# Moving the cached-key products inside four turns, and three set-up transfers to GpSimd's queue, in a hybrid decoder step

## The chip, the core and the metric

The kernel runs on one core of a Trainium2 chip, as one program with one launch. The metric is the device time of one execution in microseconds (us); the median of several executions is compared. One more execution is taken by the hardware profiler, and all rows shown here come from it.

## What is computed

The reference is one inference step of a two-layer decoder, for a prompt of 512 tokens and a sample group of 8 sequences with 8 new tokens each. Cut to what matters here:

```python
# layer 0: dilated window attention, three groups (window, dilation) = (128,1), (512,4), (2048,16)
qkv = (h @ w_qkv).reshape(B, T, 3, 3, 8, 64)            # q, k, v of three groups, 8 heads of 64
q = rope(rmsnorm(qkv[:, :, 0], q_gain), pos)
k = rope(rmsnorm(qkv[:, :, 1], k_gain), pos)
# each query sees keys at distances 0, d, 2d, .. window, in the cache and in the new tokens;
# the three groups are merged by their softmax denominators; then @ w_o
x = x + attention
x = x + (silu(h2 @ w_gate) * (h2 @ w_up)) @ w_down
# layer 1: S5 diagonal complex state-space layer, in 64 groups of 16 channels and 64 states
abar = exp(lam * dt); bbar = ((abar - 1) / lam) * bmat
x_t = abar * x_{t-1} + bbar u_t;  y = Re(C x) + D u;  out = gelu(y) @ w_glu, gated
# and a second swiglu; new caches and states are outputs too
```

## The kernel before

All activations are kept transposed (features on the 128 partitions, 576 tokens along the row), in fp32 precision: each fp32 operand is split into a high half (`whi`, rounded, by ScalarE) and a low half (`wlo`, the rest, by VectorE), and each product is three TensorE matmuls. Every weight tile `raw` that SP loads is therefore split by ScalarE and then VectorE before TensorE can use it.

**The QKV stage** (`qkv_phase`, about the first 305 us) runs nine chunks, listed in `CHUNKS` as (part, group) with part 0 = queries, 1 = keys, 2 = values. A chunk is four *turns*, numbered j = 0 to 35; a turn is one weight tile of 256 x 512 against five row banks (four of the prompt, one of the sample), and after each bank comes a *slot*. `begin()` opens a turn: it queues the loads on SP, splits the next weight, runs the work noted for this turn, and returns the split weight. `slot()` runs what was put off by `later(n, fn)`, n slots ahead. All this is written out by hand: VectorE, ScalarE, the SP queue and TensorE's inserted work are kept in program order there. GpSimd's instructions are placed by the planner (the framework's scheduler, which orders the free instructions by a timeline of its own).

After a chunk of queries or keys, the first turn of the next chunk squares its five banks (`square(t)`: a square on ScalarE into `t1`, which has two buffers, then a sum on VectorE into `sh`), one a slot; the second turn takes the root (`rsqrt`) and rotates the banks (`finish`), in the order of `TURNS`; each rotated bank is later transposed on TensorE (`turned`, L655).

Beside this, the sample group's scores against cached keys are made. Groups 0 and 1 go through TensorE (`Score`: transposes L566, `ks` copied by ScalarE, matmuls L578 and L583, then masking `row_out`). Group 2 has one key in sixteen for each query row, so it is done on VectorE: a cache tile `kc` times the query rows `qb` (both 128 x 1024, loaded by SP from the cache and from `qscr`), then a sum over the head dimension into `P2`. There are 32 such pairs, spread over turns by `PAIRS`; each is loaded one turn ahead. When the four pairs of a sequence are done, `Close2` is put off by some slots; it transposes `P2` on TensorE (L416) and masks. Its score accumulator `Sd` has one buffer. The tiles `kc` of all kinds share six buffers (`KST`).

**The first FFN** (`ffn`, about 410 to 880 us) is bound to TensorE. Between its matmul groups a generator `ssm_setup` is advanced (`tick`) that builds the tables of the state-space layer: E (GpSimd multiplies, into `ee`), W (TensorE and ScalarE), T (VectorE) and V (GpSimd, six operations for each of eight f). Each table is written to HBM; `consts(f, q)` loads the four tables of one f back by queue q. The scratch of the f loop (`cb`, `wr`) lies where `ee` was, so it can be written only when E's store is done. Here the planner orders all engines and queues. Beside the tables GpSimd multiplies the gate (`gt`, L1029) and adds the squares of the norm (`ssum`, L194). `pace` mixes copies of old cache rows to the outputs (`o_kv_s`) into the weight loads on SP. SP also carries every load of weights; four `raw` buffers hold them.

Of the kernel before, what the change touches and what calls it, by code (L numbers as in the profile page):

```python
# [8 lines left out]
F32 = mybir.dt.float32  # L9
# [4 lines left out]
OP = mybir.AluOpType  # L14
AX = mybir.AxisListType
# [19 lines left out]
CHUNKS = ((0, 2), (1, 2), (2, 2), (0, 1), (1, 1), (0, 0), (1, 0), (2, 0), (2, 1))  # L35
# [388 lines left out]
def qkv_phase(nc, tc, A, es, L):  # L424
    v, s, g, te = nc.vector, nc.scalar, nc.gpsimd, nc.tensor
# [33 lines left out]
    prods = {}  # L459
    queue, now = [], [0]  # L460

    def later(ahead, fn):
        queue.append((now[0] + ahead, fn))
# [30 lines left out]
    def close(c):  # L494
        if busy[0]:
            later(1, lambda: close(c))
        else:
            c.turn()

    busy = [False]  # L500

    def begin():
        j = turn[0]
        if 4 <= j + 2 < 36:
            part, gi = CHUNKS[(j + 2) // 4]
            raw = L["ring"].tile([128, 2, 512], F32, name="raw", bufs=4)
            kept(nc.sync.dma_start(raw, dram(A["w_qkv"], (j + 2) % 4 * 256 * 4608 + (part * 3 + gi) * 512, [[4608, 128], [128 * 4608, 2], [1, 512]])))
            raws.append(raw)
        for gi in SCORES.get(j, ()):
            b = fill[gi].pop(0)  # L510
            if gi == 1:
                cached.append((gi, b, [cache_tile(nc, A, kst, "kc", gi, b, c0, 2, 0, kept) for c0 in (0, 2)]))
            else:
                t = kst.tile([128, 2, 512], F32, name="kc")
                kept(nc.sync.dma_start(t, dram(A[CACHES[0]], b * WIN[0] * 1024, [[1024, 128], [WIN[0] * 1024, 2], [1, 512]])))
                cached.append((gi, b, [t[:, 0:1]]))
                cached.append((gi, fill[gi].pop(0), [t[:, 1:2]]))
        due = [ready.pop(0) for _ in range(PAIRS.get(j, 0))]
        for _ in range(PAIRS.get(j + 1, 0)):
            b, part = fill[2].pop(0)  # L520
            kc = cache_tile(nc, A, kst, "kc", 2, b, 2 * part, 2, 0, kept)
            qb = kst.tile([128, 2, 512], F32, name="kc")
            kept(nc.sync.dma_start(qb, dram(qscr, (b * 8 + 2 * part) * 512, [[0, 128], [512, 2], [1, 512]])))
            ready.append((b, part, kc, qb))
        if j in notes:
            notes[j]()

        if j < 4:
            split(j)
        if j >= 3:  # L530
            split(j + 1)
        for fn in works.pop(j, ()):
            fn()
        for b, part, kc, qb in due:
            if part == 0:
                prods[b] = dk.tile([128, 4, 4, 8], F32, name="P2")
                g.memset(prods[b], 0.0)
            v.tensor_tensor(kc, kc, qb, OP.mult)
            v.tensor_reduce(prods[b][:, :, 0:2, 2 * part:2 * part + 2].rearrange("p a h c -> p c a h"), kc.rearrange("p c (a h d) -> p c a h d", a=4, h=2),
                            AX.X, OP.add)  # L540
            if part == 3:
                c = Close2(nc, L, v, s, dk, psd, "Sd", prods.pop(b), b)
                later(6 if j > 31 else 10, lambda c=c: close(c))
        return splits.pop(0)

    class Score:
# [532 lines left out]
def ssm_setup(nc, tc, A, L, keep, out):  # L1079
# [26 lines left out]
    with ExitStack() as es:  # L1106
# [169 lines left out]
        with ExitStack() as e2:  # L1276
            wk = e2.enter_context(pool("sse", bufs=1))
            ee = wk.tile([128, 2, 32, 64], F32, name="ee")
            et = [wk.tile([128, 32, 8], F32, name=f"et{i}") for i in range(2)]
            g.tensor_copy(ee[:, :, :, 0], U8[:, :, 0])  # L1280
            for k in range(6):
                n = 2 ** k
                for n0 in range(0, n, 8):
                    w = min(8, n - n0)
                    bc = lambda i: U8[:, i, k][:, :, None].to_broadcast([128, 32, w])
                    cmul(g, ee[:, 0, :, n + n0:n + n0 + w], ee[:, 1, :, n + n0:n + n0 + w], ee[:, 0, :, n0:n0 + w], ee[:, 1, :, n0:n0 + w], bc(0), bc(1), et[0][:, :, :w], et[1][:, :, :w])
                yield
                yield
            yield
            g.tensor_copy(E63, ee[:, :, :, 63])  # L1290
            nc.sync.dma_start(scn["E"].rearrange("f p r q c -> p r f q c"), ee.rearrange("p r (f q) c -> p r f q c", f=8))
            yield
            yield
        with ExitStack() as e2:
# [22 lines left out]
            for f in range(8):  # L1317
                qs = slice(f * 4, f * 4 + 4)
                ps = aux.tile([128, 2, 512], F32, name="aux")
                with tc.issue_after(L["pem"][0].ins):  # L1320
                    for ri in range(2):
                        for q in range(4):
                            te.transpose(ps[:, ri, q * 128:(q + 1) * 128], wr[f][:, ri, q].rearrange("p c s -> p (c s)"), ident)
                wo = wk.tile([128, 2, 4, 128], F32, name="wo")
                s.activation(wo.rearrange("p r q c -> p r (q c)"), ps, AF.Copy)
                nc.sync.dma_start(scn["W"][f], wo)
                yield
                pk = aux.tile([128, 2, 512], F32, name="aux")
                with tc.issue_after(L["pem"][0].ins):
                    for i in range(2):  # L1330
                        for q in range(4):
                            te.matmul(pk[q * 32:q * 32 + 32, 0, :128], cb[i][:, q].rearrange("p a b -> p (a b)"), wr[f][:, i, q].rearrange("p c s -> p (c s)"),
                                      start=i == 0, stop=i == 1, tile_position=(0, q * 32), skip_group_check=True)
                kk = wk.tile([128, 128], F32, name="kk")
                v.tensor_copy(kk, pk[:, 0, :128])
                k7 = kk.rearrange("p (c s) -> p c s", s=8)[:, :, 7]
                v.scalar_tensor_tensor(k7, dmask, dcol[:, f:f + 1], k7, op0=OP.mult, op1=OP.add)
                yield
                with tc.issue_after(L["pem"][0].ins):
                    te.transpose(pk[:, 1, :128], kk, ident)  # L1340
                kt = wk.tile([128, 128], F32, name="kk")
                v.tensor_copy(kt, pk[:, 1, :128])
                st = wk.tile([128, 8, 128], F32, name="st")
                for t in range(8):
                    m = []
                    for p in range(32):
                        c, ss = divmod(p, 8)
                        m.append(c * 8 + (ss + 7 - t if ss <= t else ss))
                    v.stream_shuffle(st[:, t], kt, m)
                if f < 7:  # L1350
                    powers(f + 1)
                yield
                tt = wk.tile([128, 8, 16, 8], F32, name="wo")
                v.tensor_tensor(tt.rearrange("p g c t -> p t (g c)"), st, tmask[:, :, None].to_broadcast([128, 8, 128]), OP.mult)
                nc.sync.dma_start(scn["T"][f], tt.rearrange("p g c t -> p g (c t)"))
                vv = wk.tile([128, 8, 128], F32, name="st").rearrange("p (r q) (c t) -> p r q c t", r=2, c=16)
                vt_ = wk.tile([128, 4, 16, 8], F32, name="vt")
                pw = lambda x: x[:, 1:9, qs].rearrange("p m q -> p q m")[:, :, None, :].to_broadcast(sh)
                cb_ = lambda x: x[:, qs, :, None].to_broadcast(sh)
                p1r, p1i = pw(Ar), pw(Ai)  # L1360
                g.tensor_tensor(vv[:, 0], cb_(Cr), p1r, OP.mult)
                g.tensor_tensor(vt_, cb_(Cn), p1i, OP.mult)
                g.tensor_tensor(vv[:, 0], vv[:, 0], vt_, OP.add)
                g.tensor_tensor(vv[:, 1], cb_(Cn), p1r, OP.mult)
                g.tensor_tensor(vt_, cb_(Cr), p1i, OP.mult)
                g.tensor_tensor(vv[:, 1], vv[:, 1], vt_, OP.subtract)
                for gl in range(2):
                    for ri in range(2):
                        nc.sync.dma_start(scn["V"][f, ri, :, :, gl, :], vv[gl * 64:gl * 64 + 64, ri].rearrange("p q c t -> p q (c t)"))
                yield  # L1370
        consts(0, nc.sync)
        consts(1, nc.sync)
    kp.append(out["es"].enter_context(L["right"]("ssmk1", bufs=2)))
    consts(2, nc.sync)
    consts(3, nc.sync)


def ssm_phase(nc, tc, A, es, L, nin, sp):
# [260 lines left out]
```

## Time and profile before

| | |
|---|---|
| median of 3 runs | 1497.02 us (1496.78 to 1498.91) |
| profiled execution | 1499.43 us, of it 1497.7 us from the first to the last instruction |
| granted TensorE clock | 0.998 |
| busy share | TensorE 98%, VectorE 60%, ScalarE 35%, GpSimd 22% |
| moved by DMA | 322.64 MB, 215 GB/s over the span |
| of it by GpSimd's queue (q0, software) | 3168 packets, 7.48 MB |

How to read the rows: PE is TensorE's matmuls, PEld its weight loads, DVE is VectorE, ACT ScalarE, POOL GpSimd, SP the queue of the sync engine. `out<-in` names the tile written and those read; L12 is line 12 of the kernel; instructions that are kept in order by a wrapper all have line L760. A row of a timeline has the start, the duration, the engine, the line, the operation, the tiles with their shapes, how many, and in brackets the idle time before it with what ended it. A row of the waits has who waited for what, the total in us, the number of waits, the longest. A row of groups has the count, the busy time and the mean in ns, then the idle time before. A row of DMA issues has the size and the median us from issue to landing. A matmul's busy time reaches over the next one's start, as they are pipelined.

### The profile page before, as it was taken

To read this page: it belongs to the slowest core of one execution; us is meant where nothing else is said; L and a number is where in the kernel's file an instruction comes from. 1 tells how busy PE (TensorE), PEld (TensorE's weight loads), DVE (VectorE), ACT (ScalarE), POOL (GpSimd) and SP (SyncE) were. 2 spreads that over 40 slices of the span, in tenths; PEclk is the share of its full clock that TensorE was granted. 3 is DMA by queue.
4 is the path that set the end of the run, shared out by engine and by line. 5 is a ranking of instruction groups with operands and counts; after the bars stand their busy time and mean duration, and the time that the engine had idled before them with its cause. 6 is when DMAs were issued, how large, how long until landed. Compare 5 with 4: busy or idle time off the path is not lost. (4 is left out here: it accounts for less than half of the span.)

```text
span 1497.7 us, 29564 instructions
## 1 busy us (share of the span) xinstructions
PE 1472.2 (98%) x12406; PEld 1384.5 (92%) x12406; DVE 895.8 (60%) x1507; ACT 527.8 (35%) x814; POOL 323.1 (22%) x377
## 2 busy tenths in 40 slices
PE   9999999999999999999999999999999999999998
PEld 7888777777899999999999999899999999999998
DVE  5898988745569545388687768745443323333332
ACT  4534455465552211322223453433432212221222
POOL 2022231320030174134436520201111001100100
PEclk9999999999999999999999999999999999999999
DMA  7566788989875555677867668865555655442212
GB/s 248 209 234 229 237 278 270 365 295 348 247 252 191 204 212 204 245 238 282 288 203 246 221 219 262 232 217 168 186 197 196 223 195 195 137 138 85 83 56 81
DMA packets 191861, 322.64 MB, mean 215 GB/s; under 512 B 40016, under 2 KB 138128, under 8 KB 190320
## 3 DMA queue, kind: packets, MB, share of 16 engines
q1 hardware_dynamic: 183488, 303.24, 60.0%
q10 hardware_dynamic: 5072, 10.04, 2.0%
q0 software_dynamic: 3168, 7.48, 1.5%
q8 instruction: 97, 1.59, 0.4%
q14 instruction: 36, 0.29, 0.1%
HBM read 289.22 MB, written 118.78 MB: 272 GB/s over the span
## 5 line engine op out<-in xcount | busy, mean ns | idle before, releaser
L108 PE MATMUL acc<-xgh,wlo 128*128 128x288 f32 x1760 | 377.9, 296 | 2.2 <-DVE wlo L100 2.2
L108 PE MATMUL acc<-xgh,whi 128*128 128x288 f32 x1760 | 379.1, 297 | 0.1
L108 PE MATMUL acc<-xgl,whi 128*128 128x288 f32 x1760 | 377.7, 296 | 1.0 <-DVE xgl L174 1.0
L100 DVE TENSOR_TENSOR wlo<-raw,whi 128x1024 fp32r<-128x1024 f32 (+1 forms) x166 | 214.9, 1295 | 261.9 <-ACT whi L99 258.4
L99 ACT ACTIVATE whi<-raw 128x1024 fp32r<-128x1024 f32 (+1 forms) x166 | 172.4, 1038 | 476.2 <-PE acc L108 446.0
L108 PEld LDWEIGHTS acc<-xgh,wlo 128*128 128x128 f32 x1760 | 283.2, 188 | 2.7 <-DVE wlo L100 2.5
L108 PEld LDWEIGHTS acc<-xgl,whi 128*128 128x128 f32 x1760 | 283.1, 189 | 1.5 <-DVE xgl L174 1.3
L108 PEld LDWEIGHTS acc<-xgh,whi 128*128 128x128 f32 x1760 | 282.7, 189 | 1.5 <-issue 1.0
L1029 POOL TENSOR_TENSOR gt<-gt,rstd 128x576 f32<-128x576 f32 x44 | 72.9, 1659 | 489.3 <-ACT gt L1028 489.1
L108 PE MATMUL acc<-hh,wlo 128*128 128x288 f32 x704 | 150.8, 295 | 2.1 <-DVE wlo L100 2.1
L108 PE MATMUL acc<-hh,whi 128*128 128x288 f32 x704 | 151.6, 296 | 0.0
L108 PE MATMUL acc<-hl,whi 128*128 128x288 f32 x704 | 150.9, 295 | 0.0
L340 PE MATMUL acc<-whi,xh 128*128 128x512 f32 x288 | 118.8, 414 | 0.5 <-ACT xh L280 0.4
L108 PEld LDWEIGHTS acc<-hh,wlo 128*128 128x128 f32 x704 | 112.9, 188 | 2.3 <-DVE wlo L100 2.3
L108 PEld LDWEIGHTS acc<-hh,whi 128*128 128x128 f32 x704 | 113.0, 188 | 0.6 <-issue 0.6
L108 PEld LDWEIGHTS acc<-hl,whi 128*128 128x128 f32 x704 | 113.1, 188 | 0.0
L340 PE MATMUL acc<-wlo,xh 128*128 128x512 f32 x288 | 112.2, 391 | 0.0
L340 PE MATMUL acc<-whi,xl 128*128 128x512 f32 x288 | 111.5, 393 | 0.0
L1050 DVE TENSOR_TENSOR xT<-acc,xT 128x576 f32<-128x576 f32 x48 | 36.1, 756 | 53.5 <-PE acc L108 53.5
L194 POOL TENSOR_TENSOR ssum<-ssum,sq 128x576 f32<-128x576 f32 x21 | 36.8, 1753 | 136.2 <-ACT sq L193 106.9
L340 PEld LDWEIGHTS acc<-whi,xl 128*128 128x128 f32 x288 | 54.0, 188 | 12.0
L340 PEld LDWEIGHTS acc<-whi,xh 128*128 128x128 f32 x288 | 54.0, 188 | 11.2 <-ACT xh L280 0.9
(395 smaller groups left out, 2008.5 us busy)
## 6 DMA issues: line engine op xcount, KB each, us to landing
o_kv_s<-cache_kv_w SPq DMA_DIRECT2D x64, 1020.0 KB, 6.9
kc<-cache_kv_w SPq DMA_DIRECT2D x100, 512.0 KB, 7.4
raw<-ffn_w_gate SPq DMA_DIRECT2D x44, 512.0 KB, 3.9
raw<-ffn_w_up SPq DMA_DIRECT2D x44, 512.0 KB, 3.9
raw<-ffn_w_down SPq DMA_DIRECT2D x40, 512.0 KB, 3.5
raw<-w_qkv SPq DMA_DIRECT2D x36, 512.0 KB, 7.4
kc<-qscr SPq DMA_DIRECT2D x32, 512.0 KB, 6.7
o_kv_s<-cache_kv_w SPq DMA_DIRECT2D x16, 1008.0 KB, 6.4
```

Source lines behind the costliest of these rows:

```text
L99: s.activation(hi, raw, AF.Copy)
L100: mark[0] = v.tensor_tensor(lo, raw, hi.bitcast(F32), OP.subtract)
L108: pem[0] = te.matmul(ps[:, c, :HN], w, x[:, c * HN:(c + 1) * HN], start=first and i == 0, stop=last and i == 2)
L194: g.tensor_tensor(self.ss, self.ss, sq, OP.add)
L340: ins = nc.tensor.matmul(*a, **kw)
L1029: g.tensor_tensor(t, t, nin.r, OP.mult)
L1050: v.tensor_tensor(xv, ps[m][:, :, :HN], xv, OP.add)
```

## The change

In turns that open the chunk after one of queries or keys (j = 8, 20, 24 and 28 are those with pairs due; j = 32 is left as it was), the multiply and the sum of the due pair are put off to the fifth slot, where they come behind the fifth square. Elsewhere they stay in `begin()`. `Close2` is put off by 12 slots instead of 10 up to turn 31, and by 6 after it as before. In the set-up, the store of E, the 32 stores of V and the 16 loads of `consts(0)` to `consts(3)` are issued by GpSimd instead of SP; the stores of W and T stay on SP.

```diff
+    def products(j, due):
+        for b, part, kc, qb in due:
+            if part == 0:
+                prods[b] = dk.tile([128, 4, 4, 8], F32, name="P2")
+                g.memset(prods[b], 0.0)
+            v.tensor_tensor(kc, kc, qb, OP.mult)
+            v.tensor_reduce(prods[b][...], kc.rearrange("p c (a h d) -> p c a h d", a=4, h=2), AX.X, OP.add)
+            if part == 3:
+                c = Close2(nc, L, v, s, dk, psd, "Sd", prods.pop(b), b)
+                later(12 if j <= 31 else 6, lambda c=c: close(c))
...
-        for b, part, kc, qb in due:
...
-                later(6 if j > 31 else 10, lambda c=c: close(c))
+        if due:
+            if j % 4 == 0 and j < 32 and CHUNKS[j // 4 - 1][0] < 2:
+                later(5, lambda: products(j, due))
+            else:
+                products(j, due)
         return splits.pop(0)
...
-            nc.sync.dma_start(scn["E"].rearrange("f p r q c -> p r f q c"), ee.rearrange("p r (f q) c -> p r f q c", f=8))
+            g.dma_start(scn["E"].rearrange("f p r q c -> p r f q c"), ee.rearrange("p r (f q) c -> p r f q c", f=8))
...
-                        nc.sync.dma_start(scn["V"][f, ri, :, :, gl, :], vv[gl * 64:gl * 64 + 64, ri].rearrange("p q c t -> p q (c t)"))
+                        g.dma_start(scn["V"][f, ri, :, :, gl, :], vv[gl * 64:gl * 64 + 64, ri].rearrange("p q c t -> p q (c t)"))
...
-        consts(0, nc.sync)
-        consts(1, nc.sync)
+        consts(0, g)
+        consts(1, g)
     kp.append(out["es"].enter_context(L["right"]("ssmk1", bufs=2)))
-    consts(2, nc.sync)
-    consts(3, nc.sync)
+    consts(2, g)
+    consts(3, g)
```

More of the change, by code (lines that the diff above doesn't have):

```diff
@@ L500, in qkv_phase @@
     busy = [False]
+    def products(j, due):
[4 more added lines that the diff above has]
+            v.tensor_tensor(kc, kc, qb, OP.mult)
+            v.tensor_reduce(prods[b][:, :, 0:2, 2 * part:2 * part + 2].rearrange("p a h c -> p c a h"), kc.rearrange("p c (a h d) -> p c a h d", a=4, h=2),
+                            AX.X, OP.add)
+            if part == 3:
+                c = Close2(nc, L, v, s, dk, psd, "Sd", prods.pop(b), b)
+                later(12 if j <= 31 else 6, lambda c=c: close(c))
     def begin():
@@ L533, in begin @@
             fn()
-        for b, part, kc, qb in due:
[L535 to L542, printed above, removed]
-                later(6 if j > 31 else 10, lambda c=c: close(c))
+        if due:
[3 more added lines that the diff above has]
+                products(j, due)
         return splits.pop(0)
```

## The prediction

> **What bounds the kernel now.** I read the page's totals first, then the busy time by stage, then TensorE's waits stage by stage, and only then the timelines of the engines behind each wait. The first rows are the page's totals (busy time, share of the span, instructions), then two stages of the table of windows (PE, PEld, DVE, ACT, POOL busy; granted clock; DMA share; GB/s).
>
> ```profile
> span 1497.7 us, 29564 instructions
> ...
> PE 1472.2 (98%) x12406; PEld 1384.5 (92%) x12406; DVE 895.8 (60%) x1507; ACT 527.8 (35%) x814; POOL 323.1 (22%) x377
> ```
>
> ```profile
> 150.00:300.00 150.00, 145.75 (x1174) 112.76 (x1174) 127.94 (x189) 75.23 (x129) 38.83 (x104) 1.00 0.85 287
> 400.00:900.00 500.00, 495.66 (x3825) 491.39 (x3824) 341.14 (x618) 155.06 (x180) 190.38 (x155) 1.00 0.69 232
> ```
>
> TensorE is busy 98% of the span at full clock. Neither part of the change touches a matmul, so all that it can win is TensorE idle time: 1497.7 - 1472.2 = 25.5 us in all, of it 4.25 us in the second half of the QKV stage and 4.34 us in the first FFN with the SSM set-up. The waits of TensorE in these two stages, in that order (total, times, longest):
>
> ```profile
> PE Sd L578 <- ACT ks L760: 2.2, 2, 1.6
> PE pt L566 <- DMA kc<-cache_kv_w: 1.3, 1, 1.3
> PE pt L655 <- DVE a L760: 0.6, 1, 0.6
> ```
>
> ```profile
> PE acc L108 <- DVE wlo L100: 4.3, 2, 2.2
> ```
>
> The 2.2 us fall in turns 24 and 28 (1.6 and 0.6), the 1.3 us in turn 24, the 0.6 us in turn 22; the 4.3 us are two waits for a low half of a weight. A change here is worth at most 8.4 us, 0.56%.
>
> **Part 1: the products of cached keys in turns 8, 20, 24 and 28.** Nothing is removed. One multiply and one sum per turn move from the front of the turn to behind the sum of the fifth square. Turn 24 on VectorE, then on ScalarE (start, duration, idle before it):
>
> ```profile
> 194.24 1.23 DVE L760 TENSOR_TENSOR kc<-kc 128x1024 f32<-128x1024 f32 x1 [3.53 <-DMA kc<-qscr]
> 195.50 1.22 DVE L760 TENSOR_REDUCE P<-kc 128x16 f32<-128x1024 f32 x1
> 196.64 2.06 DVE L760 TENSOR_REDUCE sh<-t 128x8 f32<-128x512 f32 x3
> ...
> 199.91 0.68 DVE L760 TENSOR_REDUCE sh<-t 64x8 f32<-64x512 f32 x1
> 200.85 1.23 DVE L760 TENSOR_TENSOR wlo<-raw,whi 128x1024 fp32r<-128x1024 f32 x1 [0.27 <-ACT whi L760]
> ```
>
> ```profile
> 197.35 0.63 ACT L760 ACTIVATE t<-a 128x512 f32<-128x512 f32 x1 [2.88 <-DVE sh L760]
> 197.88 0.58 ACT L760 ACTIVATE ks<-pt 128x512 f32<-128x512 f32 x1
> ```
>
> VectorE stands 3.53 us before the multiply, because the query rows have not landed. The sums of squares queue behind it, the squares have two buffers, so ScalarE's third square waits 2.88 us, and the copy `ks`, next on ScalarE, comes 1.6 us late for the cached-score matmuls. With the products behind the squares, the sums start when their squares are there, `ks` no longer waits for VectorE, and that wait goes: **-1.6 us**. What is late next: the products, 1.23 + 1.22 = 2.45 us, come after the last square's sum, which ends at 200.6 today and 1.6 us earlier with that wait gone, at 199.0. That puts the low half at 201.4 instead of 200.85 and the rotation behind it 0.6 us later. The rotation's end, and the matmul that takes its result in turn 26:
>
> ```profile
> 205.30 0.68 DVE L760 TENSOR_TENSOR a<-a,rq 64x512 f32<-64x512 f32 x1
> ```
>
> ```profile
> 210.71 0.46 PE L655 MATMUL pt<-ident,a 64*128 64x64 f32 x4
> ```
>
> Today 210.7 - 206.0 = 4.7 us of cover; less 0.6 and the 1.6 us by which TensorE comes earlier, 2.5 us remain. Turn 28 is the same picture with a smaller stand:
>
> ```profile
> 234.18 1.23 DVE L760 TENSOR_TENSOR kc<-kc 128x1024 f32<-128x1024 f32 x1 [1.94 <-DMA kc<-qscr]
> ...
> 239.84 0.68 DVE L760 TENSOR_REDUCE sh<-t 64x8 f32<-64x512 f32 x1
> ```
>
> Its 0.6 us go as well: **-0.6 us**. Turn 20 is different; there VectorE has no stand to fill:
>
> ```profile
> 159.28 0.29 DVE L760 CUSTOM_DVE_ANT_0 Sall<-Sall,md 128x136 f32<-128x136 f32 x1
> ...
> 160.42 1.23 DVE L760 TENSOR_TENSOR wlo<-raw,whi 128x1024 fp32r<-128x1024 f32 x1 [0.25 <-ACT whi L760]
> ...
> 164.85 0.68 DVE L760 TENSOR_TENSOR a<-a,rq 64x512 f32<-64x512 f32 x1
> ```
>
> The order alone wins only the 0.25 us stand. The later close (12 slots instead of 10) takes the 0.29 us masking out of turn 20 and puts it behind the rotation that ends at 165.5, for which TensorE waits 0.6 us. 0.25 + 0.29 = 0.54: I take **-0.5 us**. Turn 8 has no TensorE wait near it: 0. The other closes move by two slots into slots where the score accumulator is free: 0, at worst the 0.6 us of the nearest row.
>
> The move also holds two of the six cache buffers longer. The SP queue is in order, and right behind the multiply it issues the next query rows, a weight, and the tiles for the next cached scores (rows of turn 28; then the median landing of such a tile, and TensorE's first use of it):
>
> ```profile
> 235.43 0.34 SPq L523 DMA_DIRECT2D kc<-qscr  x1
> ...
> 236.64 6.54 SPq L392 DMA_DIRECT2D kc<-cache_kv_w  x3
> ```
>
> ```profile
> kc<-cache_kv_w SPq DMA_DIRECT2D x100, 512.0 KB, 7.4
> ```
>
> ```profile
> 250.60 0.66 PE L566 MATMUL pt<-ident,kc 128*128 128x128 f32 x4
> ```
>
> In turn 28 the last sum would end at 240.5 - 0.6 = 239.9 and the multiply 1.23 us later at 241.2, against 235.4 today: 5.8 us. The first tile then goes at 236.64 + 5.8 = 242.4 and lands 7.4 us later at 249.8; TensorE wants it at 250.60 - 0.6 = 250.0. The cover is used up. Bounds: 0 if it lands by the median, 1.3 us if it is as late as the one tile that TensorE waits for today. I take **+0.3 us**, nearer the median. In turn 24 the same shift is 199.0 + 1.23 - 195.5 = 4.7 us, a us less, with that much more cover.
>
> Part 1: -1.6 - 0.6 - 0.5 + 0.3 = **-2.4 us**; ends -2.8 and, with two new tile waits of 1.3, about 0.
>
> **Part 2: E, V and constants on GpSimd's queue.** 1 + 32 + 16 = 49 DMAs leave the SP queue. One of SP's waits there (the store of V for its first half), then what ScalarE's weight halves and VectorE's products with the gate wait for, all from 400 to 900 us:
>
> ```profile
> SPq L1369 <- POOL st L1363: 20.5, 8, 5.8
> ```
>
> ```profile
> ACT whi L99 <- PE acc L108: 198.1, 54, 6.1
> ...
> DVE ut L1034 <- PE acc L108: 17.7, 17, 2.0
> ```
>
> SP loses these 20.5 us of waits for one half of V and about as much for the other, but the weights behind them are not late: ScalarE waits for TensorE to free a half, not for a weight's landing. So the relief of SP is worth 0; four weight buffers cover it. On GpSimd each DMA costs about what its present ones cost:
>
> ```profile
> L379 POOL DMA_DIRECT2D o_kv_p<-a x8 | 4.4, 556 | 15.0 <-DVE a L760 6.1 <-ACT ks L760 4.5 <-issue 2.3
> ```
>
> 49 x 0.556 = 27 us on an engine with 500 - 190 = 310 us idle. Behind these DMAs wait the gate products (VectorE never waits for them above) and the sums of squares of the norm that ends the stage. There the cover is thin:
>
> ```profile
> 876.01 2.19 POOL L194 TENSOR_TENSOR ssum<-ssum,sq 128x576 f32<-128x576 f32 x1 [1.25 <-ACT sq L193]
> ```
>
> ```profile
> 879.03 1.13 PE L199 MATMUL aux<-ssum,ones 128*128 128x288 f32 x4
> ```
>
> 878.2 against 879.0. The last eight constant loads (8 x 0.556 = 4.4 us) are queued right behind V's last table, some five adds before this one, and GpSimd idles between its adds (1.25 us before the last), so I take 0; if they fell between the last adds, up to 4.4 - 0.8 = 3.6 us lost.
>
> The place that decides is E. VectorE's next scratch lies where E was built, so it stands until E has been written (SP, then VectorE, then the high half on ScalarE, then the rows of two DMAs):
>
> ```profile
> 578.25 0.68 SPq L1291 DMA_DIRECT2D e_scr<-ee  x1
> 579.02 2.01 SPq L87 DMA_DIRECT2D raw<-ffn_w_gate  x1
> 581.09 1.35 SPq L83 DMA_DIRECT2D o_kv_s<-cache_kv_w  x1
> ```
>
> ```profile
> 587.72 0.31 DVE L1298 MEMSET cb<- 128x128 f32 x2 [4.62 <-DMA e_scr<-ee]
> ...
> 595.28 1.22 DVE L100 TENSOR_TENSOR wlo<-raw,whi 128x1024 fp32r<-128x1024 f32 x1
> ```
>
> ```profile
> 587.16 1.06 ACT L99 ACTIVATE whi<-raw 128x1024 fp32r<-128x1024 f32 x1 [5.33 <-PE acc L108]
> ```
>
> ```profile
> e_scr<-ee SPq DMA_DIRECT2D x1, 2048.0 KB, 9.3
> ...
> o_kv_s<-cache_kv_w SPq DMA_DIRECT2D x64, 1020.0 KB, 6.9
> ```
>
> E lands at 587.6; the low half that TensorE needs stands behind eight set-up operations, ends at 596.5, and TensorE waits 2.2 us. Each us that E lands earlier or later moves this wait by a us. On GpSimd's queue E still starts near 578.6, when E is computed. But SP no longer holds the weight and the cache copy behind it: they go out about 1.6 us earlier, so ahead of E. At E's own rate (2048 KB in 9.3 us, 220 KB/us) their 512 + 1020 KB are 7.0 us, less the 1.6 us head start 5.4 us. So this term lies between -2.2 (the low half is placed ahead of the memsets and the wait goes) and +5.4. [...] No run so far shows the two queues in competition for E.
>
> I take 0 for E: VectorE's order there is the planner's, worked out anew with a new queue, and the two ends pull apart. The other 2.1 us wait, at 851, is a low half stretched by V's last operations on GpSimd; I see no reason for either sign: 0, +-2.
>
> **Sum.** -2.4 + 0 = -2.4 us. The profiled execution took 1499.43 us: 1497.7 of span and 1.7 around it; its like after would be 1497.0. It stands 2.4 us above the median of 1497.02, against which the forecast is **1494.6 us**.
>
> **Rivals.** First, *the set-up's wait goes too*: the planner puts the low half before the memsets. For it: the high half is ready at 588.2, seven us before its low half runs. Against it: today's order, where it was also available. -2.4 - 2.2 = -4.6, 1492.4 us; with the wait at 851 gone as well, 1490.3.
>
> Second, the other side, *E lands late*: place 579 to 596 us, price as above. VectorE's eight operations move with E. At the full 5.4 us the total is +3.0, 1500.0 us; slower from there on, and about 1498 at half of it. For it: SP's transfers do overtake E. Against it: 5.4 supposes that they take the whole of the DMA first.
>
> Third, *the change does not do what it says*: the late release of cache buffers costs 1.3 us in two turns and the products' gain is spent: 1496.8 to 1497.
>
> **How the numbers follow.** About 0.2% (3.0 us) is what a measurement of this kernel can tell from no change: faster is below 1494.0, slower above 1500.0. The forecast case (part 1 wins, set-up within +-1.5) has 0.38, range 1493 to 1496; the first rival 0.32; the second 0.18; the third 0.12. Faster: nearly all of the first rival (0.30) and a third of the forecast case (0.12): 0.42. Slower: the upper half of the second rival (0.10) and a little for the thin cover at 879 (0.03): 0.13. Same: the rest, 0.45. The range 1490.4 to 1499.6 leaves out the far end of the second rival and the deepest gains.
>
> **What would show it.** Right: in the profile after, no TensorE wait for `ks` in turns 24 and 28, sums of squares directly behind the low half there, ScalarE's waits for `sh` gone, no gap at turn 22. E's row: its landing after the issue on GpSimd's queue, the idle time before the memsets, and TensorE's wait at the low half behind them. Wrong: new waits of TensorE for cache tiles near turns 26 and 30, for `a` in turns 26 and 30, or at L199; and in the set-up any wait for a low half over 3 us, or none at all.

## The result, and the profile after

The changed kernel takes 1505.25 us (median of 6 runs, 1501.88 to 1513.96) against 1498.03 us before (6 runs, 1496.78 to 1500.91; the three of the table above and three more): a ratio of 1.0054, 95% interval 1.0028 to 1.0079. It is slower by half a per cent, clear of the noise. The forecast was 1494.6 us and its range ended at 1499.6. The profiled execution after took 1504.42 us, of it 1502.6 us of span, 4.9 us more than the span before. Behind the new helper `products` (L502) line numbers are 7 higher than before (L767 is the former L760), in some of the experiments 1 or 2 more.

First the table of waits of TensorE after (total, times, longest): the second half of the QKV stage, then the first FFN with the set-up and the stage's end.

```profile
PE pt L573 <- DMA kc<-cache_kv_w: 1.6, 2, 1.0
PE Sd L416 <- DVE P L767: 0.4, 1, 0.4
PE pt L662 <- DVE a L767: 0.3, 1, 0.3
```

```profile
PE acc L108 <- DVE wlo L100: 8.9, 3, 5.1
PE acc L1430 <- DMA U<-u_scr: 1.9, 1, 1.9
PE acc L108 <- ACT whi L99: 0.2, 1, 0.2
```

In the QKV stage the 2.2 us for `ks` are gone, and all waits together make 2.3 us instead of 4.1. In the set-up the waits for a low half have grown from 4.3 to 8.9 us, the longest from 2.2 to 5.1. Matched matmul by matmul, TensorE is 2.4 us ahead of before at the end of the QKV stage (the same matmul starts at 303.84 us instead of 306.25) and 2.8 us from the end of the attention to the wait at 591 us. It is 1.1 us behind at 602, 1.5 from 700 on, 4.2 at 843, 3.5 at 855, 5.4 at 866 and 4.9 at the end. So the QKV part did what was forecast, and 8.2 us were lost between 591 and 866 us.

The place near 590 us: VectorE after; then TensorE's first matmul behind the wait, before; then the same matmul after, the matmuls behind it, and some when the clock is back (start, duration, idle before).

```profile
579.08 1.23 DVE L100 TENSOR_TENSOR wlo<-raw,whi 128x1024 fp32r<-128x1024 f32 x1
588.00 0.31 DVE L1305 MEMSET cb<- 128x128 f32 x2 [7.69 <-DMA e_scr<-ee]
...
595.37 1.22 DVE L100 TENSOR_TENSOR wlo<-raw,whi 128x1024 fp32r<-128x1024 f32 x1
```

```profile
596.56 0.53 PE L108 MATMUL acc<-xgh,wlo 128*128 128x288 f32 x2 [2.24 <-DVE wlo L100]
```

```profile
596.65 0.85 PE L108 MATMUL acc<-xgh,wlo 128*128 128x288 f32 x2 [5.11 <-DVE wlo L100]
597.29 0.68 PE L108 MATMUL acc<-xgh,whi 128*128 128x288 f32 x2
597.77 0.68 PE L108 MATMUL acc<-xgl,whi 128*128 128x288 f32 x2
...
602.52 0.43 PE L108 MATMUL acc<-xgh,wlo 128*128 128x288 f32 x2
602.78 0.42 PE L108 MATMUL acc<-xgh,whi 128*128 128x288 f32 x2
```

VectorE reaches the zeroing of `cb` 2.8 us earlier than before, stands 7.69 us instead of 4.62, and goes on at 588.0, nearly the same moment as before (587.7). E did not land earlier although it was issued 2.5 us earlier. TensorE came 2.8 us earlier to the low half and waits 2.9 us longer. Behind the wait a pair of matmuls starts every 0.48 us; at 602.5 us it is every 0.26 us. That is a second cost, which the table of windows shows as the granted clock (the third number from the right, ahead of the DMA share and GB/s). Windows of 3.41 us, before and then after:

```profile
594.19:597.60 3.41, 1.17 (x9) 1.04 (x9) 3.38 (x5) 0.00 (x0) 0.00 (x0) 1.00 0.00 1
597.60:601.01 3.41, 3.41 (x17) 3.41 (x16) 2.32 (x4) 1.76 (x3) 1.00 (x1) 0.50 1.22 459
601.01:604.43 3.42, 3.42 (x27) 3.42 (x27) 1.51 (x1) 0.86 (x2) 2.69 (x2) 1.00 0.15 25
```

```profile
592.19:595.60 3.41, 0.00 (x0) 0.00 (x0) 3.34 (x5) 0.00 (x0) 0.00 (x0) 1.00 0.05 19
595.60:599.01 3.41, 2.36 (x10) 2.37 (x11) 3.41 (x4) 0.00 (x0) 0.00 (x0) 0.50 0.30 80
599.01:602.43 3.42, 3.42 (x16) 3.42 (x16) 2.33 (x3) 2.21 (x3) 2.28 (x2) 0.50 0.92 379
602.43:605.84 3.41, 3.41 (x27) 3.41 (x26) 0.14 (x1) 0.68 (x1) 1.43 (x1) 1.00 1.00 359
```

Before, one window at clock 0.50 follows the wait of 2.24 us (17 matmuls in it instead of 27, about 1.7 us lost); after, two follow the wait of 5.11 us. The step near 593 us is thus 2.9 us more waiting and about 1.2 us more at half clock (6.83 us less the 1.05 us that were still idle, halved, against 3.41 halved), 4.1 in all; the matched matmuls say 3.9.

The rest lies near 843 and 866 us. VectorE there, after:

```profile
837.12 0.29 DVE L1349 COPY kk<-aux 128x128 f32<-128x128 f32 x1 [2.05 <-PE aux L1347]
840.39 0.01 DVE L1356 LOAD_MASK_SELECT st<-kk  x1 [2.97 <-DMA v_scr<-st]
...
842.05 1.22 DVE L100 TENSOR_TENSOR wlo<-raw,whi 128x1024 fp32r<-128x1024 f32 x1
```

```profile
843.33 0.53 PE L108 MATMUL acc<-hh,wlo 128*128 128x288 f32 x2 [2.52 <-DVE wlo L100]
```

```profile
841.39:844.80 3.41, 1.48 (x11) 1.48 (x12) 3.41 (x10) 0.83 (x1) 0.00 (x0) 1.00 0.08 19
844.80:848.21 3.41, 3.41 (x16) 3.41 (x16) 3.41 (x4) 2.70 (x4) 2.15 (x2) 0.50 0.76 285
```

The shuffles of T and the table V use one scratch tile, `st`. GpSimd issued the last store of V at 833.0 us, it landed 7.1 us later, and the eight shuffles with a low half behind them stood 2.97 us. TensorE waited 2.52 us and then ran one window at half clock. A further wait of 1.22 us follows at 866 us; in exchange the wait of 2.1 us at 851 us is gone: 2.5 + 1.7 + 1.2 + 0.2 - 2.1 = 3.5 us. The matched matmuls say 3.9 (from 1.5 to 5.4 behind). The 1.9 us for `U` at 904 us are given back by 994 us, where a wait of before of 1.0 us at 965 us and some of 0.3 to 0.7 us are missing.

### The profile page after: what moved, and what is told of

Same layout as the page of the kernel before. It is cut to its first block, busy times and chain, and to the rows that moved or that the text cites. A ratio compares the mean times of both kernels' runs of the same rounds, so it can differ in the third digit from the quotient of the medians.

```text
span 1502.6 us, 29577 instructions
## 1 busy us (share of the span) xinstructions
PE 1473.9 (98%) x12406; PEld 1386.6 (92%) x12406; DVE 906.7 (60%) x1507; ACT 527.9 (35%) x814; POOL 348.5 (23%) x426
## 5 line engine op out<-in xcount | busy, mean ns | idle before, releaser
L1035 ACT ACTIVATE gt<-gt 128x576 f32<-128x576 f32 x44 | 30.1, 685 | 101.8 <-DVE gt L1034 101.8
```

The source lines that it names most:

```text
L1035: s.activation(t, t, AF.Silu)
```

## The experiments

All times are medians, beside the kernel before on the same chip; the ratio with its 95% interval. The changed kernel was not run again beside them; the medians of before lie between 1497.95 and 1498.44 us in all four sets, so times of different sets are compared with the changed kernel's 1505.25 us here.

**Each part alone.** The products only, and the queues only:

```diff
 # products only: the changed kernel with
-            g.dma_start(scn["E"]...
+            nc.sync.dma_start(scn["E"]...
...
-                        g.dma_start(scn["V"]...
+                        nc.sync.dma_start(scn["V"]...
...
-        consts(0, g)
+        consts(0, nc.sync)
...
 # and so for consts(1) to consts(3); queues only: the kernel before with these edits the other way round
```

> The products behind the fifth bank and the 12 slots alone; E, V and the constants stay on SP. Theory A (the products gain what was forecast and the loss is all in the set-up): TensorE stands 2.4 to 2.8 us ahead of before at the end of the attention, E is issued by SP near 575.5 us, 2.8 us earlier than before, and lands about 9.3 us later near 585; VectorE waits for it about 4.6 us as before, TensorE's wait near 594 stays near 2.2 us, and the time is 2.4 to 2.8 us under before, about 1495.4. Rival B (the 12 slots or the changed attention also cost something that shows later, when the planner lays out the set-up anew): over 1497.5, with a new wait behind 600 us although no queue was changed.

Measured: 1496.46 us against 1498.15, ratio 0.9990 (0.9976 to 1.0004). The profiled span is 1495.0 us, 2.7 us under before. SP issues E at 576.12 us, it lands 9.2 us later, and TensorE's only waits for a low half are two of 2.1 us. Theory A holds for the trace; in the medians the gain is 1.7 us, which these runs do not quite separate from none.

> The stores of E and V and the constants by GpSimd, the products where they were. Theory A (the queue change costs by itself): E is issued at 578.3 us and lands 12.1 us later, near 590.3 instead of 587.6; TensorE's wait for wlo near 597 grows from 2.2 to about 5.0 us and the half clock behind it from 3.4 to 6.8 us, +4.5; V and the constants add about 3.8 as between 600 us and the end in the changed kernel; sum +7 to +9, about 1505.5 to 1507. Rival B (E's landing is tied to something that does not move with its issue, the end of a copy or of a weight load on SP, so that it lands near 588 whoever issues it): the wait for wlo stays near 2.3 to 2.8 us and the sum is +4 at most.

Measured: 1506.55 us, ratio 1.0058 (1.0037 to 1.0080). E is issued at 578.33 us and lands 11.9 us later, at 590.3; the waits for a low half make 8.5 us with a longest of 5.0. The whole loss is in the queues. The waits are those of theory A, and E's landing came 2.4 us later with an issue 2.6 us later. That does not yet say that the landing follows the issue: SP's cache copy ahead of E was later by as much (its first packet ended at 582.54 us instead of 579.93), so rival B's tie to a copy is open here, and the last runs below show it.

**Which of the queued transfers.** E back on SP, and E alone on GpSimd:

```diff
 # E back on SP: the changed kernel with
+            nc.sync.dma_start(scn["E"]...
 # E alone on GpSimd: the changed kernel with
+                        nc.sync.dma_start(scn["V"]...
+        consts(0, nc.sync)
...
```

> The changed kernel with E's store back on SP; V and the constants stay on GpSimd. Theory A: the wait for wlo near 594 us is about 2.2 us again, TensorE is still 2.5 us or more ahead of before at 600 us, and what V and the constants cost behind it (about 3.8 us) is left: +1 against before, about 1499. Rival B (the later waits near 843, 866 and 904 us follow from E's delay, as the planner and the pace are shifted by it): they are gone too and the time is 2.4 to 2.8 under before, 1495.4.

> The changed kernel with V and the constants back on SP; only E is stored by GpSimd. Theory A: the wait of about 5.1 us for wlo near 594 to 597 us with 6.8 us of half clock is there, the waits near 843, 866 and 904 us are not, and the time is about +1.1 against before, 1499. Rival B (the later waits come from E): they are there as in the changed kernel, and the time is near 1503 to 1505.

Measured: with E back on SP 1497.58 us, ratio 0.9991 (0.9976 to 1.0006); with E alone on GpSimd 1501.20 us, ratio 1.0024 (1.0010 to 1.0038). With E on SP, V and the constants on GpSimd cost nothing that these runs can tell from the products alone (0.9991 and 0.9990). The time lies between theory A and rival B of that run; in the trace the wait at 866 us is gone, the one at 849 us is the 2.1 us of before, and that for `U` is 0.4 us instead of 1.9, as rival B says. E alone costs its own wait, 4.5 us with 6.8 us of half clock, and the waits near 843, 866 and 904 us are not there:

```profile
PE acc L108 <- DVE wlo L100: 6.6, 2, 4.5
```

So E costs by itself, and V costs where E is on the same queue. The run with V alone taken back says the same:

```diff
 # the changed kernel with
+                        nc.sync.dma_start(scn["V"]...
```

> The changed kernel with V's stores back on SP; E and the constants stay on GpSimd. Theory A (VectorE's shuffles near 840 us wait for V's store to free st, which GpSimd issues late): the wait at 843 us is 2.1 us or less again and mostly without half clock, the one at 866 us is gone; 1505.25 less 0.4, 1.7 and 1.2, about 1502, near the 1501.2 of E alone. Rival B (the constants on GpSimd ahead of the sums of squares, 866 to 871 us, are the cost): 1504 to 1505.

Measured: 1500.44 us, ratio 1.0018 (1.0006 to 1.0030), 4.8 us under the changed kernel and near E alone. Nobody waits for V's stores any more, and of the three waits for a low half only E's is long (0.9 and 0.5 us the others):

```profile
PE acc L108 <- DVE wlo L100: 6.5, 3, 5.1
```

The constants on GpSimd are still in this kernel and cost nothing that can be seen. In the kernel with E back on SP, GpSimd issues the last store of V at 828.1 us and it lands 4.3 us later; in the changed kernel it does so at 833.0, behind a stand of its own, and it lands 7.1 us later:

```profile
830.73 0.59 POOL L1376 DMA_DIRECT2D v_scr<-st  x1 [0.29 <-POOL st L1373]
833.01 0.59 POOL L1376 DMA_DIRECT2D v_scr<-st  x1 [1.69 <-issue]
```

3.3 of these 4.9 us are TensorE's own delay since E. GpSimd stands 1.69 us in each of the four kernels with E and V on its queue; why stays open. In each of these four SP issues one of its cache copies within 0.01 us of that store (833.00 and 833.01 us here), and the store takes 6.8 to 7.7 us to land; with E back on SP, SP's next transfers follow 2.6 us behind the store. So the longer landing costs more than the stand, and a copy beside the store is likely its cause; no run here held that copy back.

**Is the price only the split behind VectorE's wait?** The zeroing of `cb` and the first powers are ordered behind the last low half queued so far, which puts three low halves ahead of them:

```diff
 # in the changed kernel, and in the products alone
+            with tc.issue_after(L["mark"][0].ins):
                 for t in cb:
                     v.memset(t, 0.0)
...
+            with tc.issue_after(L["mark"][0].ins):
                 powers(0)
```

> The changed kernel with the same order on VectorE; E is still stored by GpSimd and lands as late. Theory A (the late E costs only through the split behind VectorE's wait): the wait of 5.1 us and the half clock of 6.8 us (3.4 us) go, the waits near 843 and 866 us stay, 1505.25 - 8.5 = about 1497. Rival B (E's landing holds something else as well, such as GpSimd's next products or the set-up's transposes): half of it comes back later, 1501 or more.

Measured: 1497.74 us, ratio 0.9992 (0.9977 to 1.0006). E is still late (issued at 574.5 us, landing 11.8 us later), and no wait and no half clock is left near 590 us. The waits of V stay (2.40 us at 834 with its window at half clock). 7.5 of the forecast 8.5 us are back: E costs through VectorE's order, and little else.

> The products alone (E, V and the constants on SP), and in addition the zeroing of cb and the first powers are ordered on VectorE behind the next splits, so that VectorE does not stand for E with a split behind it. Theory A (the price of E is that VectorE's queue stands in front of the split; its wait of 2.1 us and the half clock of 3.4 us behind it, 1.7 us, are both gone): 1496.5 of the products alone less 3.8, about 1492.7. Rival B (the first powers, now later, hold up the set-up's first transposes or the splits behind them, and the wait only moves): a new wait of about 2 us behind 600 us, 1496.5.

Measured: 1494.31 us, ratio 0.9966 (0.9951 to 0.9980): the best version, faster than both kernels. The two waits of 2.1 us have become one:

```profile
PE acc L108 <- DVE wlo L100: 2.1, 1, 2.1
```

TensorE gains 4.0 us near 594 us, as forecast; 1.5 us go again near 844, where the wait of 2.1 us that is left now brings a window at half clock, which it did not in the products alone. The median shows 2.2 of the forecast 3.8 us.

**Why E takes 12 us on GpSimd.** My first theory was a slow start of that queue. E was issued by ScalarE instead, with SP's order unchanged (`himarks` lists ScalarE's splits as they are queued; the third from the end is that of about 571 us):

```diff
 # E alone on GpSimd, with
-            g.dma_start(scn["E"]...
+            with tc.issue_after(L["himarks"][-3].ins):
+                s.dma_start(scn["E"]...
```

> As E by GpSimd alone, but E is issued by ScalarE, behind the split of about 571 us and ahead of that of 578 us; SP's order is the same, with the weight and the cache copy ahead of E's store. Theory A (the long way of E is the start of GpSimd's queue: 4.2 us from issue to the first packet, where SP's took 1.2): first packet 1.2 us behind the issue, landing 9 to 9.5 us behind it near 585.3, TensorE's wait 2.1 to 2.4 us, about 1496.5. Rival B (the weight and the cache copy that SP now sends ahead hold E up, the second rival of the prediction): landing 11 to 12 us behind the issue, near 587.6, wait about 4.5 us, 1501.

Measured: 1500.04 us, ratio 1.0016 (1.0002 to 1.0031), TensorE's wait 4.0 us. Issue at 575.2 us, landing 11.2 us later, first packet at 579.92 us, 4.7 us behind the issue (SP's own store of E has its first packet 1.3 us behind the issue, in the kernel before and in the products alone). ScalarE's queue started no sooner than GpSimd's (4.7 us behind the issue, against 4.1 with E alone on GpSimd): theory A falls. What the traces have in common is the copy `o_kv_s` that SP sends ahead. It goes as 16 packets of 65280 bytes, of 2.6 to 3.7 us; E's first packet starts as the first of them ends: 579.93 and 579.93 us in the changed kernel, 582.54 and 582.55 with the queues only, 580.30 and 580.30 with E alone, 579.91 and 579.92 here. The view of DMA queues for the changed kernel, from E's issue to 579.9 us, has no packet of GpSimd's queue (q0), and 104% of the engines' time in SP's:

```profile
DMA packets 501, 1.52 MB, mean 368 GB/s; under 512 B 16, under 2 KB 485, under 8 KB 485
...
q1 hardware_dynamic: 501, 1.52, 104.0%
issues: line engine op xcount, KB each, median us to landing
e_scr<-ee POOLq DMA_DIRECT2D x1, 2048.0 KB, 12.1
```

The test is to send that one copy later (`credit` is what `pace` spends on copies):

```diff
 # in E alone on GpSimd, and in the changed kernel, one step behind E's store
+            L["credit"][0] -= 1.0
...
 # and behind the first powers
+            L["credit"][0] += 1.0
```

> As E by GpSimd alone, but the one cache copy that SP sends just ahead of E's store (at 575.0 us) goes out two weights later. In the traces so far E's first packet starts in the instant in which the first 65280-byte packet of that copy ends (579.93 and 579.93 us in the changed kernel, 580.30 and 580.30 with E alone, 579.91 and 579.92 with E by ScalarE). Theory B of the run before, now the first (the copy's long packets hold E up): the first packet of E comes within 2.5 us of the issue, E lands 8 to 9 us behind its issue, near 584.5, TensorE waits 1 to 2.2 us instead of 4.5, at most one step of half clock, 1494.5 to 1497. Theory A (GpSimd's queue starts late by itself): first packet 4.1 us behind the issue whatever is ahead, landing near 587, 1501.

Measured: 1498.57 us, ratio 0.9991 (0.9977 to 1.0005). The same view from E's issue at 577.1 us on, 3.9 us of it:

```profile
q0 software_dynamic: 153, 0.63, 46.6%
q1 hardware_dynamic: 459, 0.45, 36.3%
issues: line engine op xcount, KB each, median us to landing
e_scr<-ee POOLq DMA_DIRECT2D x1, 2048.0 KB, 8.7
```

E's first packet comes 2.00 us behind the issue, of which 1.36 us are the issue itself; E lands in 8.7 us instead of 11.4, TensorE's wait is 1.9 us instead of 4.5 and brings no half clock. The copy ahead of E was the cause. The median came out 1.6 us above the top of what was expected of it: this trace loses 1.4 us of the products' gain in the QKV stage (a cache tile late by 2.2 us with its window at half clock) and 1.8 near 938 us.

> The whole changed kernel with the same copy sent two weights later. The copy's theory: E's wait shrinks from 5.1 to about 2 us and the half clock from 6.8 to 3.4 us or none; what V costs near 843 us stays; 1505.25 less 5 to 6.5, about 1499 to 1500. The theory of the late queue: 1505.

Measured: 1500.30 us, ratio 1.0011 (0.9997 to 1.0025), 5.0 us under the changed kernel; E lands 9.6 us behind its issue. The wait is 2.7 us with no half clock, and V's wait with its half clock stays. That is what the copy's theory expected, 0.3 us above its range.

This trace also shows that the length of the copy's packets is not needed for such a delay. SP issues its next weight at 579.05 us, while E's packets of 4096 bytes, 0.23 us each on average by the view below, run on GpSimd's queue. The weight's first packet starts at 583.18 us, 4.1 us behind the issue. The view of DMA queues from 579.05 to 583.0 us has packets of q0 only:

```profile
DMA packets 284, 1.16 MB, mean 294 GB/s; under 512 B 0, under 2 KB 0, under 8 KB 284
...
q0 software_dynamic: 284, 1.16, 101.6%
issues: line engine op xcount, KB each, median us to landing
raw<-ffn_w_gate SPq DMA_DIRECT2D x1, 512.0 KB, 6.7
```

In four more kernels in which SP issues a weight while E runs, the changed one among them, it waits 3.5 to 3.7 us. In all five, 1.2 to 1.3 MB of E go first (in the changed kernel E's last 202 packets and the weight's 512 then share the engines from 583.9 us on), and 1.52 MB went ahead of E in the view of the changed kernel above. So a transfer waited for what was ahead of it, in short packets or long. For E's landing the copy's bytes are enough: 1020 KB at the 368 GB/s of that view are 2.8 us, an estimate, and without the copy E landed 2.5 to 2.7 us sooner behind its issue. A copy cut into shorter packets was not run.

## Why the prediction was wrong

**Part 1** was right: -2.4 us forecast, -2.4 us in the trace of the changed kernel at the end of the QKV stage and -2.8 by the end of the attention; -1.9 and -2.2 in the products alone, -2.7 at its end. The waits for `ks` in turns 24 and 28 went, the sums of squares run before the query rows are needed, and the products stand behind the fifth sum without a wait (VectorE after, turn 24):

```profile
196.22 0.69 DVE L767 TENSOR_REDUCE sh<-t 128x8 f32<-128x512 f32 x1 [1.14 <-ACT t L767]
...
197.44 0.68 DVE L767 TENSOR_REDUCE sh<-t 64x8 f32<-64x512 f32 x1 [0.21 <-ACT t L767]
198.04 1.21 DVE L767 TENSOR_TENSOR kc<-kc 128x1024 f32<-128x1024 f32 x1
199.28 1.22 DVE L767 TENSOR_REDUCE P<-kc 128x16 f32<-128x1024 f32 x1
200.42 1.21 DVE L767 TENSOR_TENSOR wlo<-raw,whi 128x1024 fp32r<-128x1024 f32 x1
```

The low half comes at 200.42 us, not later than before (200.85), and TensorE does not wait for the rotation behind it. Turn 22 gave 0.3 of the 0.5 us. The late tile forecast for turn 30, at 250 us, did not come; in turn 32, at 279 us, TensorE waits 0.6 us for a tile, 0.15 before. In the products alone the cache tiles cost 1.6 us more than before (2.9 against 1.3), about half of what the third rival put at stake; that the late release of buffers is what makes these tiles late was not followed.

**The step that failed is E**, taken as 0 between -2.2 and +5.4. The prediction named the place, the order on VectorE, and, in its second rival, the mechanism: SP's two transfers go out ahead of E. They did (574.18 and 574.61 us), E's landing stood still while all else came earlier, and the wait grew by 2.9 us, inside the bounds. I gave this case 0.18. For the 0 I had that the planner orders VectorE anew and that the two ends pull apart; the order did not change, the same operations stand ahead of the low half. Against the rival I had that 5.4 supposes that the two transfers take the whole of the DMA first; they did (104% of the engines' time, none of E's packets). In the table of before both transfers stand behind E's store and behind VectorE's wait nothing gives way, so the positive side should have carried the forecast. The 5.4 itself was too long because it moved the two transfers at E's own 220 KB/us: at the 368 GB/s measured while they ran, their 1.57 MB take 4.3 us, less the head start of 1.6 us 2.7, an estimate beside the 2.9 measured. E alone on GpSimd came out at 1501.20 us, above the range by itself. E by ScalarE, issued at 575.2 us while the weight's short packets still ran, did not begin among them, and SP's weights did not begin among E's packets: it was 4.7 us and 3.5 to 4.1 us from the issue to the first packet, and no run here shows why.

**A term was missing: the clock behind a wait.** A wait was priced at its length. In these traces the half clock came in windows of 3.41 us that lay on one grid from the first to the last of an execution (597.6 and 1495.3 us before: 263 windows apart; 595.6 and 1500.1 us after: 265). In the FFN, at full clock, it followed windows in which TensorE idled 1.89 us (E back on SP) to 3.41 us (after); a window with 1.77 us was not followed by it (E on GpSimd with the copy held). At half clock less was enough for another: 1.05 us of idle time after, 1.28 with E by ScalarE (0.51 with E back on SP was not). The products alone have two waits of 2.10 us; the first falls into one window, the second lies across two:

```profile
591.19:594.60 3.41, 1.31 (x10) 1.08 (x9) 3.38 (x5) 0.00 (x0) 0.00 (x0) 1.00 0.01 3
594.60:598.01 3.41, 3.41 (x16) 3.41 (x15) 2.89 (x4) 1.08 (x2) 0.33 (x1) 0.50 1.27 460
...
843.77:847.18 3.41, 2.82 (x22) 2.58 (x20) 3.41 (x3) 1.02 (x2) 3.41 (x2) 1.00 0.45 146
847.18:850.59 3.41, 1.90 (x14) 1.90 (x15) 3.39 (x4) 1.25 (x2) 3.33 (x3) 1.00 0.41 109
850.59:854.00 3.41, 3.41 (x28) 3.41 (x27) 3.16 (x2) 2.09 (x3) 3.41 (x2) 1.00 0.53 154
```

With E back on SP the wait of 2.10 us near 849 us falls into one window, and costs 1.7 us more:

```profile
846.69:850.10 3.41, 1.31 (x10) 1.07 (x9) 3.41 (x4) 0.53 (x2) 3.41 (x2) 1.00 0.00 0
850.10:853.51 3.41, 3.41 (x16) 3.41 (x16) 3.22 (x3) 2.82 (x3) 3.41 (x5) 0.50 0.93 238
```

So the price of a wait near 2 us was its length and, by the grid's place, 0 or 1.7 us; a wait of 2.7 us across two windows also brought none (the changed kernel with the copy held), and the five waits of 4.0 to 5.1 us brought two windows each. It is likely a part of the spread of the runs: the slowest of after, 1513.96 us, had a mean clock of 0.990, the profiled one, 1504.42 us, 0.996; 0.006 of 1510 us are 9.1 us, their difference is 9.5. It is not all of it: the run at 0.991 took 1508.04 us, 3.6 us more than the profiled one where the clock would give 7.5.

**"27 us on GpSimd, hidden"** was right as busy time (323.1 to 348.5 us) and wrong as cover: I looked at who waits for GpSimd's engine, and not at who waits for the landing of what it stores. V's scratch is also the shuffles' scratch. This term, put at 0, is the other 3.9 us of the trace (1.5 to 5.4 behind), and it was in no rival. The thin cover at 879 us held: no wait at L199 after.

**The first rival**, the low half ahead of the zeroing, did not happen by itself. Ordered by hand, beside the products alone, the trace is 5.0 us under before, the rival's 4.6 with some half clock; the medians show 3.6.

## What to carry to other kernels

When a store moves to another queue, look at what the old queue will send in its place: what gets ahead on the DMA engines went first in every trace here, 1.2 to 1.5 MB of it, 3.5 to 4.7 us from the issue to the first packet. For every table that is stored, list who reuses its scratch, since here its landing and not its issue freed it (12.1 us behind the issue for E, 7.1 us for V's last store before the shuffles). Price a wait of TensorE near 2 us, where TensorE is the bound, with the slower clock that may stand behind it (0 or 1.7 us here, 2.9 us behind the wait of 5.11 us), and put work that waits for a store behind the work that TensorE needs.

## What was not expected of the hardware

E's first packet waited for the end of a 65280-byte packet in flight, from two different queues (4.2 us behind GpSimd's issue, 4.7 us behind ScalarE's; 2.00 us with the copy out of the way); and SP's weights waited as long, 3.5 to 4.1 us, behind E's packets of 4096 bytes. In the FFN, where a window held one wait and little else, TensorE's clock halved for 3.41 us behind windows with 1.89, 1.93, 2.10 and 2.24 us of idleness; 1.77 us in a window, and 2.10 us across two windows, did not do it. Idle time alone is not the whole of it: near 938 us, where the matmuls are smaller, 1.51 us in a window did it too (E on GpSimd with the copy held).
